# Layer B's channel-major products with the high and low halves side by side, and large tiles at multiples of 1024 bytes

## The chip, the core and the metric

The kernel runs on one core of a Trainium2 chip. A core has five engines that run their own instruction streams: TensorE (PE, matrix products into PSUM; its weight loads are shown as PEld), VectorE (DVE), ScalarE (ACT), GpSimd (POOL) and SyncE (SP, which issues the DMAs here). The metric is the device time of one execution in microseconds (us). The program is recorded through a tile layer which puts each engine's instructions in an order of its own making before they are built; each engine then runs its list strictly in that order and waits on semaphores.

## What is computed

A decoder trunk with two layers for 256 positions and a model width of 2048. Layer A is a Mamba-2 mixer. Behind it, one shared set of keys and values is made from the residual stream `x`. Layer B is a dilated windowed attention with three head groups, whose merged output is gated and projected. Only this part matters here:

```
x = layer A's output                                  # 256 x 2048
k, v = split(x @ kv_w, 2)                             # kv_w 2048 x 6144
h = x * (1 + scale) + shift                           # adaLN from c
q, z = split(h @ b_in_w, [3072])                      # b_in_w 2048 x 4096
o = merge of the three groups' attention(q, k, v)     # 256 x 1024
o = o * silu(z)
out = layer_norm(alpha * x + (1 + gate) * (o @ b_out_w))
```

All arrays are float32. TensorE's fast type for this is `float32r`, which keeps fewer bits, so the kernel splits each operand into a high half (`hi`, rounded to `float32r`) and a low half (`lo`, the remainder), and computes a product as three: hi·hi + hi·lo + lo·hi.

## The kernel before

**Weights.** Each weight matrix is laid out in pieces of 128 partitions x 1024 values (0.5 MB). `load_piece` (L84) issues the DMA of a piece into `raw` (6 buffers); `split` (L89) lets ScalarE copy it to `whi` (L92) and VectorE subtract to `wlo` (L94), 3 buffers each. In `wkv` and `wbin` a piece holds 512 columns for two row tiles of 128 (k = 2).

**Channel-major products.** `cm_quad` (L128) computes 512 output columns with channels on the partitions: 8 pieces, through `cm_piece` (L108). For each of the 16 row tiles and each of 4 blocks of 128 columns it issues three matmuls, all with 256 moving columns (the positions):

```
T.matmul(o, hi[:, k, c_], ahi[:, kt, :], ...)    # L118
T.matmul(o, hi[:, k, c_], alo[:, kt, :], ...)    # L119
T.matmul(o, lo[:, k, c_], ahi[:, kt, :], ...)    # L120
```

So a quad is 192 matmuls, each with a weight load of its own. Its four results lie in two PSUM tiles of 128 x 2 x 256, which ScalarE copies out with one 128x512 instruction each. **Token-major products** (`tm_chunk`, L152 to L154) have the activations as weights and `whi`/`wlo` as the moving operand, 512 columns at a time.

**The stages around the change**, with their place in the profiled execution (us from the span's start, read from the evictions and the matmuls):
- 560 to 743: layer A's output product (`tm_chunk` on `wout`, 768 matmuls of 512 columns), whose weights are `yhi` (tile name `actT`) and `ylo`; then layer norm.
- 758 to 826: `cm_quads` makes the keys of the first half of the heads, while `x_tiles` writes `xhi` and `xlo` (also `actT`).
- 826 to 904: three `cm_quad`s make the second half's keys, with `background(4, 9)`: four of layer B's adaLN columns (`araw`: a DMA of 1 MB and a dot product of 2.3 us on VectorE, L218) for every nine pieces.
- 904 to 1035: the values (`tm_chunk`). Then `xhi`/`xlo` are overwritten by the split of h.
- 1035 to 1262: `queries(0)`, `attend(0)`, `queries(1)`, `attend(1)`, `z_gate(0)`, `z_gate(1)` in program order: 6 + 2 quads on `wbin`. The tile layer moves matmuls of the next quad between those of `attend`, as filling.
- 1262 to the end: the output product on `wbout`, layer norm, and the output's DMAs.

Of the 26 quads' worth of channel-major work in the kernel, 11 are touched: 3 in the second keys' stage and 8 on `wbin`.

**Evictions**: `evict_k` (L665) and `queries` (L719) copy on ScalarE, two instructions for a quad; `z_gate` (L763) applies SiLU straight from PSUM, then VectorE multiplies (L764), and `split_act` splits the gated output on ScalarE (L175) and VectorE (L176) for the output product.

**Buffers and addresses.** The pool `act` has two buffers of 16 KB a partition, which hold in turn `hhi`/`hlo`, `yhi[0]`/`yhi[1]`, `xhi`/`xlo`, `gt`/`lnt`. In the program as built, `raw`, `whi`, `wlo` and `actT` start 128 bytes past a multiple of 1024; `ylo`, `kk`, `vt`, `qq` and the late split tiles `hi`/`lo` (L800) start 256 bytes past one. The split output of attention lies in the `kk` and `vt` buffers.

Of the kernel before, what the change touches and what calls it, by code (L numbers as in the profile page):

```python
# [9 lines left out]
F32 = mybir.dt.float32  # L10
F32R = mybir.dt.float32r
I32 = mybir.dt.int32
AF = mybir.ActivationFunctionType
ALU = mybir.AluOpType
# [4 lines left out]
P = 128  # L19
L = 256  # L20
D = 2048
KT = D // P
# [26 lines left out]
@with_exitstack  # L49
def trunk(ctx, tc, xT, x, c, par, cst, bias, lnrow, ada, wdt, win, wout, wkv, wbin, wbout, out):  # L50
    nc = tc.nc
# [3 lines left out]
    wp = ctx.enter_context(tc.tile_pool(name="wp", bufs=3))  # L55
    act = ctx.enter_context(tc.tile_pool(name="act", bufs=2))
    sm = ctx.enter_context(tc.tile_pool(name="sm", bufs=2))
# [12 lines left out]
    nc.sync.dma_start(prm, par)  # L70
    cc = cons.tile([P, NCONST], F32, name="cc")

    def pv(name):
# [58 lines left out]
    def cm_quad(src, ahi, alo, rate=(0, 1), k0=0):  # L132
# [4 lines left out]
        return ps  # L137

    def tiles(ps):
        return [ps[n // 2][:, n % 2, :] for n in range(4)]  # L140
# [37 lines left out]

    sm.tile([P, 40], F32, name="pad", bufs=1)
    magic = cons.tile([P, 2], I32, name="magic")  # L180
# [69 lines left out]

    hhi = act.tile([P, KT, L], F32R, name="actT")
    hlo = act.tile([P, KT, L], F32R, name="actT")

    with ExitStack() as cA:
# [14 lines left out]
        with ExitStack() as cS:  # L269
# [63 lines left out]
            with ExitStack() as c0:  # L333
# [73 lines left out]
                for i, (k, q) in enumerate(order):  # L407
# [5 lines left out]
                    z = k >= 0 and kinds[k] == "z"  # L413
# [152 lines left out]
        pn = cA.enter_context(tc.tile_pool(name="pn", bufs=1, reuse_waits="tile"))  # L566
        yhi = [act.tile([P, KT, L], F32R, name="actT") for _ in range(2)]
        ylo = {g: pn.tile([P, 4, L], F32R, name=f"ylo{g}") for g in (0, 1, 2, 3, 4, 7, 5, 6)}
# [68 lines left out]

    xhi, xlo = (act.tile([P, KT, L], F32R, name="actT") for _ in range(2))
    pb = ctx.enter_context(tc.tile_pool(name="pb", bufs=1))
# [23 lines left out]
    def evict_k(hq, g, ps):  # L663
        for w in range(2):
            S.activation(kk[hq][:, g, 2 * w:2 * w + 2, :], ps[w], AF.Copy)  # L665

    with ExitStack() as cL:
# [9 lines left out]
        with tc.issue_after(nb_last.ins):  # L677
            queue(pl, cols1[16:])
            jobs.append(lambda: gate_out(1))
            for g in range(NG):  # L680
                evict_k(1, g, cm_quad(wkv[2 * g + 1], xhi, xlo, rate=R))
            for hq in range(2):
                for g in range(NG):
                    ps = tm_chunk(wkv[6 + 2 * g + hq], hx, lx, rate=R)
                    for b in range(2):
                        S.activation(vt[hq][:, g, b, :], ps[b], AF.Copy)
            drain()
# [26 lines left out]
    def queries(hq):  # L714
        qq = pc2.tile([P, 12, L], F32, name="qq").rearrange("p (g i) l -> p g i l", g=NG)
        for g in range(NG):
            ps = cm_quad(wbin[2 * g + hq], xhi, xlo, rate=R)
            for w in range(2):
                S.activation(qq[:, g, 2 * w:2 * w + 2, :], ps[w], AF.Copy)  # L719
        return qq  # L720
# [39 lines left out]
    def z_gate(hq, qq):  # L760
        pz = cm_quad(wbin[6 + hq], xhi, xlo, rate=R)
        for w in range(2):
            S.activation(qq[:, 1, 2 * w:2 * w + 2, :], pz[w], AF.Silu)  # L763
        V.tensor_tensor(qq[:, 0], qq[:, 0], qq[:, 1], op=ALU.mult)  # L764
# [13 lines left out]

    gt = act.tile([P, 2, D], F32, name="actT")
    bcast(gt[:, 0, :], gated[1])  # L780
    lnt = act.tile([P, 2, D], F32, name="actT")
    for i in range(2):
# [53 lines left out]
def _layout(x, c, ada_w, ada_b, ln_g, ln_b, a_in_w, a_conv_w, a_conv_b, a_dt_bias,  # L836
# [27 lines left out]
    for g, (win_, dil) in enumerate(((128, 1), (512, 4), (2048, 16))):  # L864
# [13 lines left out]
        "ada": ada, "wdt": _dt(dt), "win": win,  # L878
        "wout": _pieces(a_out_w[0]), "wkv": _pieces(kv_w), "wbin": _pieces(b_in_w[0]), "wbout": _pieces(b_out_w[0]),
    }  # L880
# [20 lines left out]
```

## Time and profile before

| | before |
|---|---|
| median of 3 runs | 1321.53 us (1319.25 to 1325.56) |
| the profiled execution | 1324.63 us, of it the span of all instructions 1322.8 us |
| mean granted TensorE clock | 0.989 |
| channel-major matmuls, L118, L119, L120 | 1664 each, mean 285 to 287 ns |
| DMA traffic | 335.94 MB, mean 254 GB/s |

How to read it: a matmul's duration covers its whole way through the array, so that neighbours overlap; what a matmul costs in a dense stretch is the distance from its start to the next one's start, which is called its pitch here. In a table of windows, each engine's column gives the busy time and, behind x, the number of instructions that touch the window. In a group's row the busy time and the mean duration stand first, then the engine's idle time just before those instructions and what ended it.

### The profile page before, as it was taken

The numbers are of one execution on the slowest core, as the hardware profiler recorded it, in microseconds if no ns is written. First come the engines' busy times: TensorE is split into PE (matmuls) and PEld (weight loads), VectorE is DVE, ScalarE is ACT, GpSimd is POOL, SyncE is SP. The second block draws the span as 40 slices with busy tenths as digits, with TensorE's granted clock in tenths as the row PEclk, the third lists the DMA queues.
The fourth block names the chain that finished last, engine by engine and source line by source line (L and its number), as shares of the span: only waits on it lengthen the run. The fifth ranks groups of instructions, "written<-read, shape, count | busy, mean of one in ns | idle before, by whom it ended". The sixth has DMA issues, their size and how long they took to land.

```text
span 1322.8 us, 20650 instructions
## 1 busy us (share of the span) xinstructions
PE 1255.0 (95%) x8082; PEld 1133.5 (86%) x8082; DVE 1013.2 (77%) x1403; ACT 700.1 (53%) x1000; POOL 26.6 (2%) x20
## 2 busy tenths in 40 slices
PE   3799999999999999999999799999999999999995
PEld 3689988899989899777888699998888999999984
DVE  6889786999996788889765577877877647648577
ACT  3354478757766677854333444444445545445451
POOL 0000000000000000000000043000000000000000
PEclk9999999999999999999999899999999999999998
DMA  9999757777856555488966574898897553352471
GB/s 386 423 421 421 285 211 256 263 263 286 303 202 228 175 176 176 158 285 329 400 224 207 195 236 166 318 405 339 342 392 282 210 186 116 126 190 84 157 271 64
DMA packets 80450, 335.94 MB, mean 254 GB/s; under 512 B 8960, under 2 KB 9056, under 8 KB 67552
## 3 DMA queue, kind: packets, MB, share of 16 engines
q1 hardware_dynamic: 80352, 334.62, 68.1%
q8 instruction: 63, 1.03, 0.3%
q14 instruction: 35, 0.29, 0.1%
HBM read 332.41 MB, written 2.18 MB: 253 GB/s over the span
## 4 chain that ended last, share of the span: by engine, by line
PE 79%; DVE 10%; DMA 5%; ACT 3%; issue 2%; SPq 0%; ACTq 0%; DVEq 0%
PE acc L120 13%; PE acc L118 13%; PE acc L119 13%; PE acc L153 12%; PE acc L154 11%; PE acc L152 11%; DMA araw<-in_ada 4%; DVE wlo L94 3%; DVE araw L218 2%; PE py L530 2%; PE aux L732 1%; DVE cacc L287 1%; ACT whi L92 1%; PE po L756 1%; PE po L746 1%
## 5 line engine op out<-in xcount | busy, mean ns | idle before, releaser
L94 DVE TENSOR_TENSOR wlo<-raw,whi 128x1024 fp32r<-128x1024 f32 x394 | 486.1, 1241 | 239.0 <-ACT whi L92 236.2
L92 ACT ACTIVATE whi<-raw 128x1024 fp32r<-128x1024 f32 x394 | 414.9, 1057 | 415.7 <-PE acc L119 185.8
L118 PE MATMUL acc<-actT,whi 128*128 128x256 f32 x1664 | 474.5, 287 | 5.9 <-ACT whi L92 4.4
L120 PE MATMUL acc<-actT,wlo 128*128 128x256 f32 x1664 | 472.4, 287 | 6.2 <-DVE wlo L94 6.0
L119 PE MATMUL acc<-actT,whi 128*128 128x256 f32 x1664 | 472.9, 285 | 0.0
L118 PEld LDWEIGHTS acc<-actT,whi 128*128 128x128 f32 x1664 | 321.4, 194 | 8.3 <-ACT whi L92 5.6
L120 PEld LDWEIGHTS acc<-actT,wlo 128*128 128x128 f32 x1664 | 319.8, 193 | 9.1 <-DVE wlo L94 8.9
L119 PEld LDWEIGHTS acc<-actT,whi 128*128 128x128 f32 x1664 | 321.4, 193 | 0.5
L152 PE MATMUL acc<-whi,actT 128*128 128x512 f32 x704 | 272.0, 395 | 22.4 <-ACT actT L361 20.1
L153 PE MATMUL acc<-wlo,actT 128*128 128x512 f32 x704 | 278.6, 396 | 4.4 <-DVE wlo L94 4.3
L218 DVE SCALAR_TENSOR_TENSOR araw<-araw,cb__72 128x2048 f32<-128x2048 f32 x96 | 219.4, 2287 | 14.7 <-DMA araw<-in_ada 14.5
L152 PEld LDWEIGHTS acc<-whi,actT 128*128 128x128 f32 x704 | 133.0, 190 | 51.2 <-ACT actT L361 20.1
L154 PE MATMUL acc<-whi,actT 128*128 128x512 f32 x448 | 175.1, 391 | 0.0
L153 PEld LDWEIGHTS acc<-wlo,actT 128*128 128x128 f32 x704 | 132.6, 188 | 35.9 <-DVE wlo L94 8.3
L154 PE MATMUL acc<-whi,ylo 128*128 128x512 f32 x256 | 102.2, 400 | 0.0
L154 PEld LDWEIGHTS acc<-whi,actT 128*128 128x128 f32 x448 | 84.4, 188 | 16.8
L154 PEld LDWEIGHTS acc<-whi,ylo 128*128 128x128 f32 x256 | 48.0, 188 | 9.6
L287 DVE SCALAR_TENSOR_TENSOR cacc<-acc,prm,cacc 128x253 f32<-128x253 f32 (+2 forms) x96 | 42.3, 477 | 7.9 <-ACT cacc L284 7.5
L489 ACT ACTIVATE seg<-cbc,cumT 128x128 f32<-128x128 f32 x128 | 40.6, 388 | 11.5 <-PE py L530 11.5
L530 PEld LDWEIGHTS py<-xd,seg 128*128 128x128 f32 x256 | 30.7, 192 | 6.5 <-DVE xd L502 3.6
L530 PE MATMUL py<-xd,seg 128*128 128x64 f32 x256 | 30.5, 273 | 2.0 <-DVE xd L502 2.0
L702 POOL TENSOR_TENSOR u<-u,lnr 128x512 f32<-128x512 f32 x8 | 13.3, 1686 | 795.2 <-DMA lnr<-in_lnrow 763.7
(196 smaller groups left out, 927.0 us busy)
## 6 DMA issues: line engine op xcount, KB each, us to landing
araw<-in_ada SPq DMA_DIRECT2D x96, 1024.0 KB, 7.5
raw<-in_win SPq DMA_DIRECT2D x160, 512.0 KB, 5.0
raw<-in_wkv SPq DMA_DIRECT2D x96, 512.0 KB, 6.5
raw<-in_wout SPq DMA_DIRECT2D x64, 512.0 KB, 4.6
raw<-in_wbin SPq DMA_DIRECT2D x64, 512.0 KB, 3.3
cbc<-cumd SPq DMA_DIRECT2D x16, 512.0 KB, 5.4
raw<-in_wbout SPq DMA_DIRECT2D x16, 512.0 KB, 3.8
xt<-in_xT SPq DMA_DIRECT2D x8, 256.0 KB, 10.2
```

The source lines that it names most:

```text
L92: S.activation(hi, raw, AF.Copy)
L94: latest[0] = V.tensor_tensor(lo, raw, hi.bitcast(F32), op=ALU.subtract)
L118: T.matmul(o, hi[:, k, c_], ahi[:, kt, :], start=first, stop=False, skip_group_check=True)
L119: T.matmul(o, hi[:, k, c_], alo[:, kt, :], start=False, stop=False, skip_group_check=True)
L120: T.matmul(o, lo[:, k, c_], ahi[:, kt, :], start=False, stop=kt == k1 - 1, skip_group_check=True)
L152: T.matmul(ps[b], h_, hi[:, k, :], start=kt == k0, stop=False)
L153: T.matmul(ps[b], h_, lo[:, k, :], start=False, stop=False)
L154: T.matmul(ps[b], l_, hi[:, k, :], start=False, stop=kt == k1 - 1)
L218: V.scalar_tensor_tensor(raw, raw, 1.0, cb_, op0=ALU.mult, op1=ALU.mult, accum_out=mod[layer][:, ct, j:j + 1])
L287: V.scalar_tensor_tensor(acc[:, o:], ps[:, :L - o], w[:, j:j + 1], acc[:, o:], op0=ALU.mult, op1=ALU.add)
L489: S.activation(seg[:, hh, b, :], cbc[:, hh, b, :], AF.Relu, bias=cumT[:, b, h0 + hh:h0 + hh + 1], scale=-1.0)
L530: T.matmul(py[:, e_], segs[hh // 4][:, hh % 4, b, :], xd[:, b, e_], start=True, stop=True)
```

## The change

Three things are changed together.

1. A new `cm_wide` replaces `cm_quad` in the second keys' stage, in `queries` and in `z_gate`. It computes 256 output columns (a quad becomes two of them). `xhi` and `xlo` lie side by side in one tile `xp`, so that one matmul with `hi` as weights streams both (512 moving columns) into the two halves of a PSUM tile; a second one adds lo·hi (256 columns) to the first half. For 64 pairs a quad, three matmuls become two. The two halves must then be added: for each of the two PSUM tiles ScalarE copies one half out (128x256) and VectorE adds the other (128x256). `z_gate` applies SiLU afterwards, on the sum in SBUF.
2. The pieces for it hold 256 columns for four row tiles (`_pieces(w, 256, 4)`), as many bytes as before; the second keys' weights become an input of their own, `wk1`.
3. The pool `act` gets one buffer of 32 KB in place of two of 16 KB, with tiles that hold both halves; a pad of 896 bytes in `cons` and a smaller one in `sm` move the large tiles. As built, `raw`, `whi`, `wlo`, `actT`, `y`, `ylo`, `kk`, `vt`, `qq`, `hi`/`lo` all start at multiples of 1024 bytes.

The two programs' instruction lists as built have the same order on each engine up to the end of the first keys' stage. SP's list is the same throughout but for the source of the second keys' pieces.

```diff
-    act = ctx.enter_context(tc.tile_pool(name="act", bufs=2))
+    act = ctx.enter_context(tc.tile_pool(name="act", bufs=1))
...
+    cons.tile([P, 224], F32, name="pad")
...
+    def cm_wide(src, dst, rate=(0, 1)):
+        ps = acc_pair()
+        for q in range(KT // 4):
+            hi, lo = (t.rearrange("p k n -> p (k n)").rearrange("p (k n) -> p k n", k=4)
+                      for t in split(load_piece(src[q])))
+            for k in range(4):
+                kt = 4 * q + k
+                for n in range(2):
+                    c_ = slice(n * P, n * P + P)
+                    T.matmul(ps[n], hi[:, k, c_], xp[:, kt], start=kt == 0, stop=False, skip_group_check=True)
+                    T.matmul(ps[n][:, 0, :], lo[:, k, c_], xhi[:, kt, :], start=False, stop=kt == KT - 1,
+                             skip_group_check=True)
+            background(*rate)
+        for n in range(2):
+            S.activation(dst[:, n, :], ps[n][:, 1, :], AF.Copy)
+            V.tensor_tensor(dst[:, n, :], ps[n][:, 0, :], dst[:, n, :], op=ALU.add)
...
-    sm.tile([P, 40], F32, name="pad", bufs=1)
+    sm.tile([P, 8], F32, name="pad", bufs=1)
...
-    hhi = act.tile([P, KT, L], F32R, name="actT")
-    hlo = act.tile([P, KT, L], F32R, name="actT")
+    hp = act.tile([P, 2, KT, L], F32R, name="actT")
+    hhi, hlo = hp[:, 0], hp[:, 1]
...
-        yhi = [act.tile([P, KT, L], F32R, name="actT") for _ in range(2)]
+        yp = act.tile([P, 2, KT, L], F32R, name="actT")
+        yhi = [yp[:, 0], yp[:, 1]]
...
-    xhi, xlo = (act.tile([P, KT, L], F32R, name="actT") for _ in range(2))
+    xp = act.tile([P, KT, 2, L], F32R, name="actT")
+    xhi, xlo = xp[:, :, 0, :], xp[:, :, 1, :]
...
-                evict_k(1, g, cm_quad(wkv[2 * g + 1], xhi, xlo, rate=R))
+                for w in range(2):
+                    cm_wide(wk1[2 * g + w], kk[1][:, g, 2 * w:2 * w + 2, :], rate=R)
...
-            ps = cm_quad(wbin[2 * g + hq], xhi, xlo, rate=R)
             for w in range(2):
-                S.activation(qq[:, g, 2 * w:2 * w + 2, :], ps[w], AF.Copy)
+                cm_wide(wbin[2 * (2 * g + hq) + w], qq[:, g, 2 * w:2 * w + 2, :])
...
-        pz = cm_quad(wbin[6 + hq], xhi, xlo, rate=R)
         for w in range(2):
-            S.activation(qq[:, 1, 2 * w:2 * w + 2, :], pz[w], AF.Silu)
+            z = qq[:, 1, 2 * w:2 * w + 2, :]
+            cm_wide(wbin[2 * (6 + hq) + w], z)
+            S.activation(z, z, AF.Silu)
...
-    gt = act.tile([P, 2, D], F32, name="actT")
+    gl = act.tile([P, 2, 2, D], F32, name="actT")
+    gt, lnt = gl[:, 0], gl[:, 1]
...
-    lnt = act.tile([P, 2, D], F32, name="actT")
...
-        "wout": _pieces(a_out_w[0]), "wkv": _pieces(kv_w), "wbin": _pieces(b_in_w[0]), "wbout": _pieces(b_out_w[0]),
+        "wout": _pieces(a_out_w[0]), "wkv": _pieces(kv_w), "wbin": _pieces(b_in_w[0], 256, 4),
+        "wk1": _pieces(kv_w[:, :3072].reshape(D, 3, 2, 512)[:, :, 1].reshape(D, 1536), 256, 4), "wbout": _pieces(b_out_w[0]),
```

More of the change, by code (lines that the diff above doesn't have):

```diff
@@ L49, in trunk @@
 @with_exitstack
-def trunk(ctx, tc, xT, x, c, par, cst, bias, lnrow, ada, wdt, win, wout, wkv, wbin, wbout, out):
+def trunk(ctx, tc, xT, x, c, par, cst, bias, lnrow, ada, wdt, win, wout, wkv, wk1, wbin, wbout, out):
     nc = tc.nc
```

## The prediction

> **What bounds the kernel now.** I read the page first: its busy shares, its slices and the chain.
>
> ```profile
> PE 1255.0 (95%) x8082; PEld 1133.5 (86%) x8082; DVE 1013.2 (77%) x1403; ACT 700.1 (53%) x1000; POOL 26.6 (2%) x20
> GB/s 386 423 421 421 285 211 256 263 263 286 303 202 228 175 176 176 158 285 329 400 224 207 195 236 166 318 405 339 342 392 282 210 186 116 126 190 84 157 271 64
> PE 79%; DVE 10%; DMA 5%; ACT 3%; issue 2%; SPq 0%; ACTq 0%; DVEq 0%
> ```
>
> TensorE is busy 95% of the span and holds 79% of the chain that ended last. A 95% says nothing yet about the stages that are changed, so I asked for the busy times by stage: the first three rows are the second keys' stage (it ends at 904), the others run from the first query products to the last gate product.
>
> ```profile
> core 0: us, PE busy (x) PEld busy (x) DVE busy (x) ACT busy (x) POOL busy (x), PEclk, DMA share, GB/s
> 826.00:840.00 14.00, 13.36 (x112) 13.16 (x111) 11.15 (x11) 8.54 (x11) 0.00 (x0) 1.00 0.79 273
> 840.00:860.00 20.00, 19.60 (x164) 19.40 (x163) 17.82 (x16) 6.27 (x7) 0.00 (x0) 1.00 0.90 348
> 860.00:904.00 44.00, 44.00 (x366) 43.91 (x366) 34.54 (x31) 19.07 (x20) 0.00 (x0) 1.00 0.95 380
> ...
> 1037.00:1103.00 66.00, 66.00 (x552) 66.00 (x551) 29.78 (x26) 26.58 (x28) 0.00 (x0) 1.00 0.57 198
> 1103.00:1142.00 39.00, 38.93 (x277) 35.26 (x276) 33.45 (x89) 19.80 (x41) 0.00 (x0) 1.00 0.26 94
> 1142.00:1194.00 52.00, 52.00 (x435) 52.00 (x434) 22.49 (x19) 21.36 (x23) 0.00 (x0) 1.00 0.49 174
> 1194.00:1238.00 44.00, 43.90 (x317) 39.86 (x316) 34.79 (x90) 20.94 (x43) 0.00 (x0) 1.00 0.26 90
> 1238.00:1262.00 24.00, 24.00 (x203) 24.00 (x202) 13.04 (x11) 11.62 (x12) 0.00 (x0) 1.00 0.52 188
> ```
>
> In these rows TensorE idles 1.2 us in all, at full granted clock (1.00). So what a matmul less is worth is its pitch. VectorE is the second in line: 89% (17.82 of 20) while the adaLN columns are worked off, 86% and 79% under `attend`, 45% (29.78 of 66) in the plain query products. A saving on TensorE is real in the last kind of stage, and can be eaten by VectorE in the first two.
>
> The pitch comes from dense windows of one kind each:
>
> ```profile
> 930.00:1010.00 80.00, 80.00 (x354) 66.15 (x353) 65.39 (x59) 33.72 (x35) 0.00 (x0) 1.00 0.91 361
> 640.00:740.00 100.00, 100.00 (x435) 81.84 (x434) 58.14 (x56) 38.40 (x37) 0.00 (x0) 1.00 0.71 253
> 1040.00:1100.00 60.00, 60.00 (x502) 60.00 (x501) 26.10 (x23) 24.34 (x25) 0.00 (x0) 1.00 0.56 193
> 1270.00:1284.00 14.00, 14.00 (x62) 11.36 (x61) 12.27 (x14) 8.60 (x9) 0.00 (x0) 1.00 0.87 332
> ```
>
> About two of each count began before the window. The 256-column matmuls of the queries (third row): 60 / 500 = 120 ns. The 512-column ones of the values (first row): 80 / 352 = 227 ns. From the two: 107 ns for each 256 columns, and 13 ns for each matmul whatever its width (2 x 120 - 227 = 13). The two other rows are the output products of layers A and B: 100 / 433 = 231 ns and 14 / 60 = 233 ns, for the same shape as the 227.
>
> **The change part by part.**
>
> *Fewer, wider matmuls.* The streamed columns stay the same (512 + 256 in place of 3 x 256). In each of 11 quads x 64 pairs = 704 places one matmul and its weight load go, so 704 x 13 ns = 9.2 us, with the unrounded 2 x 120 - 226.7 = 13.3 ns 9.4 us. By stage: 3 quads in the second keys' stage, 192 x 13.3 = 2.5 us; 8 quads on `wbin`, 512 x 13.3 = 6.8 us. What the trace does not show is a 512-column matmul and a 256-column one in turn, with a weight load under each. Bounds: a pair costs 227 + 120 = 347 ns if each keeps its pitch, 360 if the fixed parts do not fall, and 320 (3 x 107) if they vanish, so 0 to 28 us are saved; a loss I leave out, since three matmuls in a row added to one place of PSUM before as well. I take 347: in the 120 ns stretches a weight load fits under a 256-column matmul already, and the same loads stand under both shapes.
>
> The Trainium skill, "TensorE: Matmul & The Clock Gate", section "Back-to-back issue gap", gives for a warm clock N / 2.4 + 2.5 ns from one matmul's start to the next, that is a fixed part of 2.5 ns where the rows above show 13. By it the 704 matmuls would be worth 1.8 us. The row's 13 decides.
>
> *Evictions.* For a quad two ScalarE copies of 128x512 from PSUM go; four of 128x256 and four VectorE additions come. Nearest rows: the copy in `queries`, a ScalarE copy of 128x256 out of PSUM, VectorE on 128x256 out of PSUM.
>
> ```profile
> L719 ACT ACTIVATE qq<-acc 128x512 f32<-128x512 f32 x12 | 7.0, 587 | 7.3 <-PE acc L120 7.3
> L752 ACT ACTIVATE pT<-po 128x256 f32<-128x256 f32 x16 | 6.1, 381 | 9.5 <-PE po L746 9.5
> L758 DVE COPY qq<-po 128x256 f32<-128x256 f32 x8 | 3.4, 423 | 5.8 <-PE po L757 5.7
> L94 DVE TENSOR_TENSOR wlo<-raw,whi 128x1024 fp32r<-128x1024 f32 x394 | 486.1, 1241 | 239.0 <-ACT whi L92 236.2
> L92 ACT ACTIVATE whi<-raw 128x1024 fp32r<-128x1024 f32 x394 | 414.9, 1057 | 415.7 <-PE acc L119 185.8 <-PE acc L154 177.7 <-DMA raw<-in_win 17.1
> L218 DVE SCALAR_TENSOR_TENSOR araw<-araw,cb__72 128x2048 f32<-128x2048 f32 x96 | 219.4, 2287 | 14.7 <-DMA araw<-in_ada 14.5
> L218 DVE DVE_READ_ACCUMULATOR araw<-araw,cb__72 128x1 f32 x96 | 8.0, 84 | 0.0
> ```
>
> ScalarE: 4 x 0.38 - 2 x 0.59 = +0.3 us a quad. VectorE: 4 x 0.42 = +1.7 us a quad. Behind each wide product the lists as built have: copy, weight split, copy on ScalarE; addition, split, addition on VectorE. When the product ends, two further pieces are already split, 2 x 16 matmuls x 173 ns = 5.5 us of TensorE work. The third piece's `lo` is ready after 0.4 (copy) + 1.06 (`whi`) + 1.24 (`wlo`) + 0.2 allowed for the steps between engines = 2.9 us. So in the query and gate stages the evictions cost nothing; 2.6 us of slack hide them. Each wide product has its own pair of PSUM tiles and the next one 11 us of work (64 x 173 ns), so no accumulator is late either.
>
> *Second keys' stage.* Here VectorE has, over 24 pieces, 24 x 1.24 + some 11 columns x 2.37 (the dot product and its accumulator's read) + 12 x 0.42 = 61 us, against 192 x 0.347 = 66.6 us of TensorE, and each of the six pairs of additions stands in line with the splits behind it: VectorE waits there for the product's end and two copies, up to 0.9 us each time. That is 61 + 5 = 66, no slack at all. Bounds: nothing lost if the additions find the product finished, 6 x 0.9 = 5.4 us if each wait comes in full. I take 1.5 us, since after 860 VectorE had 9 of 44 us free. The DMA queue carries the same bytes in 4% less time: 380 x 1.04 = 395 GB/s, below the 421 to 423 of the second to fourth slices.
>
> *Under `attend`.* VectorE gets about two additions in each of the two stages. ScalarE gets two more table loads: in the list as built the first SiLU stands between the exponentials of the last head, with a load before it and one behind.
>
> ```profile
> L763 ACT ACT_TABLE_LOAD  x1: 1283/1283/1283, 1237.8 to 1237.8; - x1
> L763 ACT ACTIVATE qq<-acc x4: 579/597/597, 1239.1 to 1263.6; 128x512 f32<-128x512 f32 x4
> ```
>
> That puts 2 x 1.28 + 0.6 = 3.2 us ahead of the last exponential. In front of the transposes that wait for it TensorE's list has 33 wide matmuls (33 x 173 ns = 5.7 us) where it had 27 narrow ones (3.2 us), so nearly all of it is hidden; the splits behind it on ScalarE are what could be late. From 0 to 3.2 us plus 4 x 0.42; I take 0.8 us for both `attend` stages.
>
> *The last gate.* Its chain to the output product was: SiLU twice (one split between them), multiply, split.
>
> ```profile
> 1262.07 0.60 ACT L763 ACTIVATE qq<-acc 128x512 f32<-128x512 f32 x1 [1.22 <-PE acc L120]
> ...
> 1267.81 1.22 DVE L176 TENSOR_TENSOR vt<-qq,kk 128x1024 fp32r<-128x1024 f32 x1
> ```
>
> 7.0 us, just covered by the first half of the output product. Now a copy, an addition and a VectorE split enter: 0.42 + 0.42 + 1.24 less the SiLU and wait they replace; by the lists some 7.7 us. I take 0.6 us (0 to 2).
>
> *Addresses.* Where moving operand and weights start at the same remainder of 1024 bytes, the 512-column pitch is 227 (`whi` and `actT`, both 128). Where they differ it is 231 to 233: `whi` 128 against `ylo` 256 in layer A's output product, and against `kk`/`vt` 256 in the first half of layer B's. Behind the change all are at 0. If the difference is the cause, 768 x 4 + 96 x 6 ns = 3.6 us go. Bounds: 0, if it is something else about those products, and a loss if the common remainder 0 is a bad one (a rival). I take 3.5.
>
> The Trainium skill, "SBUF — State Buffer", section "Who interferes with whom", gives TensorE two independent read ports, one for the moving operand and one for the weights, and lets it wait for nobody; by that the addresses would change nothing. No run here shows yet which holds.
>
> *Nothing else moves.* The order up to the end of the first keys' stage is the same on every engine; the single `act` tile is reused only after products that read both halves to their end.
>
> **The sum.** -9.4 - 3.5 + 1.5 + 0.8 + 0.6 = -10.0 us. The profiled execution took 1324.63 us (span 1322.8 and 1.8 around it), 3.1 over the median of the runs; 1324.6 would become 1314.6, and the median 1321.53 becomes **1311.5 us**, 0.76% less.
>
> **Rivals.**
> 1. *Addresses do nothing*: what slows the two output products is something else about them, and it stays: 1311.5 + 3.5 = 1315.0. For it: only two products show it. Against: all rows of this shape sort by the remainder. 12%. (The independent ports of the Trainium skill's "SBUF — State Buffer" would have it so.)
> 2. *The fixed part does not fall*: a narrow matmul behind a wide one takes 133 ns and a pair 360, so 1311.5 + 9.4 = 1321. For it: no such pair is in the trace. Against: the 13 ns stand under both widths. 6%. (By the Trainium skill's 2.5 ns a matmul it would be 1319.)
> 3. *VectorE takes TensorE's place* in the second keys' stage and under `attend`: with 5.4 for 1.5 and 3.2 + 1.7 for 0.8, so 1311.5 + 8 = 1319.5. For it: 89% and 86% busy before the additions come. 12%.
> 4. *Slower.* Bringing all tiles to one remainder makes moving reads and weight loads collide in every product, by the 4 to 6 ns that the unequal pairs show. The split products have these matmuls:
>
> ```profile
> L118 PE MATMUL acc<-actT,whi 128*128 128x256 f32 x1664 | 474.5, 287 | 5.9 <-ACT whi L92 4.4
> L152 PE MATMUL acc<-whi,actT 128*128 128x512 f32 x704 | 272.0, 395 | 22.4 <-ACT actT L361 20.1
> ```
>
>    3 x 1664 + 3 x 704 - 704 = 6400, x 6 ns = 38 us on top of rival 1's 1315: 1353. It is slower by more than 0.5% from 2.0 ns a matmul (6.5 that the rest gains and 6.6, over 6400). Against: pairs with equal remainders are the fast ones. 5%.
> 5. *Faster by far:* addresses also set the 13 ns; half of it gone is 6400 x 6.5 = 42 us, 1270. Against: at equal remainders 128 and 256 the pitch is the same, 227. 3%.
>
> **How the numbers follow.** The forecast has 62%, from 1304 (no costs, and runs as spread as before) to 1317. About 0.5% (6.6 us) is what a measurement tells from no change. Faster: nearly all of the forecast, half of rival 1, rival 5: 67%. Same: the rest of 1 and 2 and most of 3: 26%. Slower: 4 and the worst of 3: 7%. The range 1304 to 1320 takes in the forecast, rival 1 and part of 3, and leaves out about 20%.
>
> **What would show it.** Right: pairs of L152 and L153 at 227 and 120 ns; a `wbin` quad 22.2 us long in place of 23.0; layer A's output product at 227 ns a matmul, so 3 us shorter; VectorE near 95% between 830 and 860 with TensorE idle for 2 to 3 us; two table loads more. Wrong: a pitch of 133 behind a wide matmul (rival 2), gaps on TensorE released by `wlo` or the additions in every quad (rival 3), or the first layer's pitches of 120 and 227 moved at all (rivals 4 and 5).

## The result, and the profile after

| | before | after |
|---|---|---|
| median | 1322.61 us (1319.25 to 1325.56, 6 runs) | 1312.99 us (1310.91 to 1315.7, 6 runs) |
| ratio | | 0.9929, 95% interval 0.991 to 0.9949 |
| profiled execution, its span | 1324.63, 1322.8 us | 1312.58, 1310.8 us |

The changed kernel is 0.7% faster; the forecast was 1311.5 us, with a range from 1304 to 1320. First the page of the changed kernel: busy shares, the chain that ended last (its first row), and the groups that answer to those shown of before. Line numbers are each kernel's own; `cm_quad`'s matmuls are now L120 to L122, the wide ones L152 and L153, those of the output products L173 to L175.

```profile
PE 1241.7 (95%) x7378; PEld 1091.6 (83%) x7378; DVE 1027.8 (78%) x1447; ACT 704.7 (54%) x1028; POOL 26.4 (2%) x20
PE 77%; DVE 10%; DMA 6%; ACT 4%; issue 3%; SPq 0%; ACTq 0%; DVEq 0%
L120 PE MATMUL acc<-actT,whi 128*128 128x256 f32 x960 | 272.6, 287 | 6.2 <-ACT whi L94 4.7
L152 PE MATMUL acc<-actT,whi 128*128 128x512 f32 x704 | 250.1, 397 | 0.0
L153 PE MATMUL acc<-actT,wlo 128*128 128x256 f32 x704 | 201.3, 286 | 0.9 <-DVE wlo L96 0.9
```

There are 704 matmuls fewer (8082 less 7378), TensorE is busy 13 us less, and its share of the span is 95% as before: the kernel has become shorter along with its bound. The last row also says that the wide products waited 0.9 us for low halves in the whole run, so the additions on VectorE did not become the bound.

Where the time went is read from instructions that mark the stages; these rows give the first and the last start of each group. Before:

```profile
L577 PE MATMUL aux<-cc,y x64: 270/272/332, 557.9 to 607.1; 128*128 128x128 f32 x64
L646 PE MATMUL aux<-cc,u x32: 270/272/476, 755.8 to 815.3; 128*128 128x128 f32 x32
L665 ACT ACTIVATE kk<-acc x12: 576/597/598, 826.4 to 903.6; 128x512 f32<-128x512 f32 x12
L686 ACT ACTIVATE vt<-acc x12: 573/600/602, 924.7 to 1034.8; 128x512 f32<-128x512 f32 x12
L152 PE MATMUL acc<-whi,kk x32: 390/393/404, 1262.6 to 1284.3; 128*128 128x512 f32 x32
```

And after:

```profile
L599 PE MATMUL aux<-cc,y x64: 270/272/332, 556.0 to 605.5; 128*128 128x128 f32 x64
L669 PE MATMUL aux<-cc,u x32: 270/272/474, 751.7 to 811.3; 128*128 128x128 f32 x32
L688 ACT ACTIVATE kk<-acc x6: 577/589/598, 822.4 to 829.8; 128x512 f32<-128x512 f32 x6
L157 ACT ACTIVATE kk<-acc x12: 365/384/386, 840.7 to 897.6; 128x256 f32<-128x256 f32 x12
L710 ACT ACTIVATE vt<-acc x12: 572/598/599, 919.1 to 1029.2; 128x512 f32<-128x512 f32 x12
L173 PE MATMUL acc<-whi,kk x32: 389/389/504, 1250.7 to 1272.4; 128*128 128x512 f32 x32
```

From the marks come the lengths of the stages. The table gives them for the experiments too, from the same marks in their traces (us):

| | up to the last `y` transpose | layer A's output product | first keys | second keys | values | queries, attend, gates | output product to the end |
|---|---|---|---|---|---|---|---|
| before | 607.1 | 148.7 | 70.6 | 77.1 | 131.2 | 227.8 | 60.3 |
| after | 605.5 | 146.2 | 70.7 | 75.2 | 131.6 | 221.5 | 60.1 |
| e1 wide, old addresses | 604.3 | 148.7 | 70.8 | 75.8 | 131.6 | 221.1 | 60.6 |
| e2 addresses alone | 603.9 | 146.3 | 71.5 | 76.3 | 131.2 | 227.8 | 59.8 |
| e3 three narrow, new layout | 604.6 | 146.3 | 71.4 | 78.6 | 131.2 | 226.8 | 60.2 |
| e5 two wide, two narrow | 605.0 | 146.3 | 70.8 | 74.3 | 131.6 | 219.9 | 61.5 |
| e7 without the additions | 605.8 | 146.2 | 70.9 | 74.2 | 131.6 | 220.9 | 59.8 |
| e8 one SiLU | 604.1 | 146.2 | 70.8 | 75.8 | 131.6 | 221.8 | 60.1 |
| e9 by piece | 606.1 | 146.2 | 70.7 | 74.9 | 131.6 | 220.1 | 59.8 |
| e10 the change again | 605.6 | 146.2 | 71.4 | 74.9 | 131.7 | 221.3 | 60.1 |
| e12 unequal remainders | 604.7 | 148.7 | 71.1 | 76.5 | 131.6 | 221.5 | 60.6 |

Read the first column first: no instruction in it is changed by any of these kernels (about 52 of the 256 `ylo` products of layer A start in it, whose changed addresses are worth some 0.2 us there), and yet it varies by 3 us (by 4 with the kernels not in the table), about as much as the runs of one kernel do. Layer A's output product, the values and the queries' stage repeat to 0.1 to 0.7 us where the instructions are the same. The first keys vary by 1.1 us, and the second keys, with VectorE near its limit, by 1.6: 74.9 to 76.5 in after, e1, e8, e10 and e12, which issue the same instructions there. So most stages tell more here than a median, but each is one execution, and a difference in the second keys' stage has to be large to count. Of the 12.0 us by which the span fell, 1.6 lie in the first column; the rest is 10.4, of it 2.5 in layer A's output product, 2.0 (before rounding) in the second keys' stage, and 6.3 in the queries, `attend` and the gates.

Windows in dense stretches of the changed kernel: layer A's output product, the first queries, the second ones.

```profile
core 0: us, PE busy (x) PEld busy (x) DVE busy (x) ACT busy (x) POOL busy (x), PEclk, DMA share, GB/s
640.00:740.00 100.00, 100.00 (x443) 82.81 (x442) 59.38 (x56) 39.22 (x37) 0.00 (x0) 1.00 0.78 257
1040.00:1090.00 50.00, 50.00 (x285) 43.37 (x284) 25.42 (x28) 21.67 (x28) 0.00 (x0) 1.00 0.64 194
1143.00:1182.00 39.00, 39.00 (x227) 34.41 (x226) 19.46 (x21) 16.57 (x21) 0.00 (x0) 1.00 0.62 189
```

In the first row 443 matmuls stand where 435 stood: less the two that began before, 100 / 441 = 227 ns. The two others have the same shapes and the same clock, 1.00, and yet differ. The evictions give the pair's pitch exactly, since from the first copy of one wide product to that of the third after it lie 96 pairs. Copies between 1050 and 1086, and between 1150 and 1185:

```profile
L157 ACT ACTIVATE qq<-acc x7: 374/383/383, 1051.1 to 1085.0; 128x256 f32<-128x256 f32 x7
```

```profile
L157 ACT ACTIVATE qq<-acc x7: 378/383/385, 1151.2 to 1184.5; 128x256 f32<-128x256 f32 x7
```

33.9 / 96 = 353 ns, and 33.3 / 96 = 347 ns. The 347 is the sum of the forecast's 227 + 120. The 353 was in no part of it. A stretch of the trace at 353 shows how a pair divides; columns are the start, the duration, and the matmul:

```profile
1050.21 0.40 PE L152 MATMUL acc<-actT,whi 128*128 128x512 f32 x1
1050.45 0.28 PE L153 MATMUL acc<-actT,wlo 128*128 128x256 f32 x1
1050.57 0.40 PE L152 MATMUL acc<-actT,whi 128*128 128x512 f32 x1
1050.81 0.28 PE L153 MATMUL acc<-actT,wlo 128*128 128x256 f32 x1
1050.92 0.40 PE L152 MATMUL acc<-actT,whi 128*128 128x512 f32 x1
1051.16 0.28 PE L153 MATMUL acc<-actT,wlo 128*128 128x256 f32 x1
1051.28 0.40 PE L152 MATMUL acc<-actT,whi 128*128 128x512 f32 x1
```

The narrow matmul starts 0.24 us behind the wide one, and the next wide one 0.11 to 0.12 later. In the mean of these stretches the two distances are 237 and 117 ns where a pair takes 353 (1050 to 1085), and 230 and 117 ns where it takes 347 (1145 to 1182). So neither part has its price of the prediction's dense windows, only the 347 has their sum, and what grows in the slower pattern is the distance behind the wide matmul.

### The profile page after: what moved, and what is told of

Its sections match the earlier page's. It is cut to its first block, busy times and chain, and to the rows that moved or that the text cites. A ratio compares the mean times of both kernels' runs of the same rounds, so it can differ in the third digit from the quotient of the medians.

```text
span 1310.8 us, 19308 instructions
## 1 busy us (share of the span) xinstructions
PE 1241.7 (95%) x7378; PEld 1091.6 (83%) x7378; DVE 1027.8 (78%) x1447; ACT 704.7 (54%) x1028; POOL 26.4 (2%) x20
## 4 chain that ended last, share of the span: by engine, by line
PE 77%; DVE 10%; DMA 6%; ACT 4%; issue 3%; SPq 0%; ACTq 0%; DVEq 0%
PE acc L152 11%; PE acc L174 11%; PE acc L175 11%; PE acc L173 11%; PE acc L122 7%; PE acc L120 7%; PE acc L121 7%; PE acc L153 6%; DMA araw<-in_ada 5%; DVE wlo L96 3%; DVE araw L239 2%; PE py L551 2%; DVE cacc L308 1%; ACT whi L94 1%; PE aux L755 1%
## 5 line engine op out<-in xcount | busy, mean ns | idle before, releaser
L173 PE MATMUL acc<-whi,actT 128*128 128x512 f32 x704 | 271.6, 394 | 22.8 <-ACT actT L382 20.6
L120 PE MATMUL acc<-actT,whi 128*128 128x256 f32 x960 | 272.6, 287 | 6.2 <-ACT whi L94 4.7
L122 PE MATMUL acc<-actT,wlo 128*128 128x256 f32 x960 | 269.8, 286 | 5.1 <-DVE wlo L96 5.0
L121 PE MATMUL acc<-actT,whi 128*128 128x256 f32 x960 | 271.6, 284 | 0.0
L152 PE MATMUL acc<-actT,whi 128*128 128x512 f32 x704 | 250.1, 397 | 0.0
L153 PE MATMUL acc<-actT,wlo 128*128 128x256 f32 x704 | 201.3, 286 | 0.9 <-DVE wlo L96 0.9
L120 PEld LDWEIGHTS acc<-actT,whi 128*128 128x128 f32 x960 | 185.6, 194 | 8.3 <-ACT whi L94 5.9
L122 PEld LDWEIGHTS acc<-actT,wlo 128*128 128x128 f32 x960 | 183.6, 193 | 7.2 <-DVE wlo L96 7.2
L121 PEld LDWEIGHTS acc<-actT,whi 128*128 128x128 f32 x960 | 185.6, 193 | 0.4
L175 PE MATMUL acc<-whi,actT 128*128 128x512 f32 x448 | 175.1, 391 | 0.0
L173 PEld LDWEIGHTS acc<-whi,actT 128*128 128x128 f32 x704 | 132.0, 188 | 50.8 <-ACT actT L382 20.6
L152 PEld LDWEIGHTS acc<-actT,whi 128*128 128x128 f32 x704 | 132.1, 188 | 29.3
L153 PEld LDWEIGHTS acc<-actT,wlo 128*128 128x128 f32 x704 | 133.2, 189 | 2.4 <-DVE wlo L96 1.7
L175 PE MATMUL acc<-whi,ylo 128*128 128x512 f32 x256 | 100.5, 393 | 0.0
L175 PEld LDWEIGHTS acc<-whi,actT 128*128 128x128 f32 x448 | 84.4, 188 | 16.8
L175 PEld LDWEIGHTS acc<-whi,ylo 128*128 128x128 f32 x256 | 48.0, 188 | 9.6
```

The lines of the kernel that those rows point to most:

```text
L120: T.matmul(o, hi[:, k, c_], ahi[:, kt, :], start=first, stop=False, skip_group_check=True)
L121: T.matmul(o, hi[:, k, c_], alo[:, kt, :], start=False, stop=False, skip_group_check=True)
L122: T.matmul(o, lo[:, k, c_], ahi[:, kt, :], start=False, stop=kt == k1 - 1, skip_group_check=True)
L152: T.matmul(ps[n], hi[:, k, c_], xp[:, kt], start=kt == 0, stop=False, skip_group_check=True)
L153: T.matmul(ps[n][:, 0, :], lo[:, k, c_], xhi[:, kt, :], start=False, stop=kt == KT - 1, skip_group_check=True)
L173: T.matmul(ps[b], h_, hi[:, k, :], start=kt == k0, stop=False)
```

## The experiments

All ratios are to the kernel before, run beside the experiment on the same chip.

**e1 and e2: each half of the change alone.** e1 is the changed kernel with the tiles at their old remainders (128 and 256 past a multiple of 1024 bytes):

```diff
-    cons.tile([P, 224], F32, name="pad")
...
-    sm.tile([P, 8], F32, name="pad", bufs=1)
+    sm.tile([P, 40], F32, name="pad", bufs=1)
```

> The change without its pads, so that the large tiles keep the remainders of the kernel before (128 bytes for the split weights and xp, 256 for ylo and the kk and vt buffers). Theory (704 matmuls fewer at 13.3 ns each, and the output products slowed by unequal remainders): about 1316 us, with layer A's output product at 231 ns a matmul as before and the wide pairs at 347 to 354 ns. Rival (addresses do nothing): 1313 us as the full change, and the output product at 227. Rival (the addresses do all of it): 1321 us.

Measured: 1316.35 us, ratio 0.9949 (0.9932 to 0.9966). Its window in layer A's output product has the old count, and the wide pairs are as in the changed kernel:

```profile
640.00:740.00 100.00, 100.00 (x435) 81.84 (x434) 57.46 (x55) 38.40 (x37) 0.00 (x0) 1.00 0.74 249
1040.00:1090.00 50.00, 50.00 (x285) 43.31 (x284) 25.83 (x28) 21.07 (x28) 0.00 (x0) 1.00 0.64 190
```

e2 is the kernel before with the two pads of the change and nothing else:

```diff
+    cons.tile([P, 224], F32, name="pad")
...
-    sm.tile([P, 40], F32, name="pad", bufs=1)
+    sm.tile([P, 8], F32, name="pad", bufs=1)
```

> The kernel before with only the two pads changed, so that all large tiles start at multiples of 1024 bytes; every product is narrow. Theory: 1322.6 - 3.5 = about 1319 us, layer A's output product at 227 ns a matmul in place of 231, and the narrow products at 120 as before. Rival (addresses do nothing): 1322.6 and 231. Rival (the multiples of 1024 make every product faster): below 1315.

Measured: 1319.63 us, ratio 0.997 (0.9959 to 0.9981). Here the output product has the new count, and the narrow matmuls keep their pitch of 50 / 417 = 120 ns:

```profile
640.00:740.00 100.00, 100.00 (x443) 82.81 (x442) 58.10 (x55) 39.20 (x37) 0.00 (x0) 1.00 0.73 253
1040.00:1090.00 50.00, 50.00 (x419) 50.00 (x418) 20.83 (x17) 20.86 (x22) 0.00 (x0) 1.00 0.57 184
```

The halves work on different matmuls and add up: 0.51% and 0.30% make 0.81%, with the whole at 0.71% (0.51 to 0.9). Rival 1 (addresses do nothing) and rival 4 (a common remainder collides) have fallen.

**e3: the new layout without the wide matmul.** Everything of the change stays, the evictions with additions too; only the 512-column matmul becomes two of 256.

```diff
-                    T.matmul(ps[n], hi[:, k, c_], xp[:, kt], start=kt == 0, stop=False, skip_group_check=True)
+                    T.matmul(ps[n][:, 0, :], hi[:, k, c_], xhi[:, kt, :], start=kt == 0, stop=False, skip_group_check=True)
+                    T.matmul(ps[n][:, 1, :], hi[:, k, c_], xlo[:, kt, :], start=False, stop=kt == KT - 1, skip_group_check=True)
```

> The changed kernel, with three matmuls of 256 columns again in the place of the 512 and the 256, into the same halves of PSUM; pieces, additions, addresses and tiles as in the change. Theory (what is gained lies in the fixed part of each matmul): 704 x 13 ns come back less the 6 ns by which part of the pairs run above 347, so 7 to 9 us above the change, 1320 to 1322, at 120 ns a matmul. Rival (the gain is of the new pieces, the evictions or the order): within 2 us of 1313.

Measured: 1319.01 us, ratio 0.997 (0.9959 to 0.9982), as e2. So by the medians the layout, the pieces of four row tiles and the new evictions cost nothing that the runs resolve, and what the changed kernel has on top is the wide matmul. The stages of the two traces say 1.7 us more for e3 than for e2 (+2.3, -1.0 and +0.4), but e3's profiled execution, 1320.92 us, lay 1.9 above its median and e2's, 1318.59 us, 1.0 below. By the medians the wide matmul is then worth 4 to 5 us: the changed kernel is 9.6 us below its own before, and 8.7 when run again (e10), where e3 is 4.5 below its own; the spread of the runs leaves that uncertain by some 3 us. In the second keys' stage (window 831 to 900) TensorE waits for low halves 2.0 us, as the row shows; in the changed kernel it was 0.9.

```profile
L154 PE MATMUL acc<-actT,wlo 128*128 128x256 f32 x184 | 52.5, 285 | 2.0 <-DVE wlo L96 2.0
```

**e4 and e12: which addresses matter.** e4 is the kernel before with other pads, so that all large tiles start 256 bytes past a multiple of 1024 (one execution):

```diff
+    cons.tile([P, 32], F32, name="pad")
...
-    sm.tile([P, 40], F32, name="pad", bufs=1)
+    sm.tile([P, 8], F32, name="pad", bufs=1)
```

> The kernel before with pads that put the split weights, the activations, ylo, kk and vt all 256 bytes past a multiple of 1024: equal remainders, but no multiples of 1024. Theory (unequal remainders slow a product): layer A's output product at 227 ns a matmul. Rival (only multiples of 1024, or of 512, are good): it stays at 231. Rival (chance decides which pattern a product falls into): either, with no rule.

Measured: 1322.09 us, and in the window that decides:

```profile
640.00:740.00 100.00, 100.00 (x443) 82.80 (x442) 60.02 (x57) 39.09 (x37) 0.00 (x0) 1.00 0.77 260
```

443 again. A common remainder is enough; multiples of 1024 have no merit of their own. (The single time says little: its first stretch alone took 608.0 us, 4.1 more than e2's; from there on the two spans differ by 0.6 us.) e12 goes the other way: the changed kernel with 128 bytes more ahead of `ylo`, `kk` and `vt`.

```diff
-    sm.tile([P, 8], F32, name="pad", bufs=1)
+    sm.tile([P, 40], F32, name="pad", bufs=1)
```

> The changed kernel with 128 bytes more ahead of the tiles of layer A's output operand, the keys and the values: these begin at 128 past a multiple of 1024 again, the weights and layer B's moving operand stay at 0. Theory (a difference of the two operands' remainders costs 4 to 6 ns on a 512-column matmul): layer A's output product goes from 227 back to 231 (435 matmuls in 100 us in place of 443) and the first half of layer B's from 227 to 231 or more, 3.5 us: 1316.5. Rival (only the remainders 128 beside 256 cost, 0 beside 128 does not; or it is not the addresses): 227 stays and the time stays at 1313.

Measured: 1315.93 us, ratio 0.995 (0.9937 to 0.9964).

```profile
640.00:740.00 100.00, 100.00 (x434) 81.88 (x433) 57.28 (x54) 38.39 (x37) 0.00 (x0) 1.00 0.72 246
```

100 / 432 = 231 ns: the loss is back with remainders 0 and 128 as it was with 128 and 256.

The 231 is a mean over unlike matmuls. In layer A's output product only every third matmul has unequal remainders, the one with `ylo` as weights (L154 of the kernel before):

```profile
659.78 0.39 PE L152 MATMUL acc<-whi,actT 128*128 128x512 f32 x1
660.00 0.40 PE L153 MATMUL acc<-wlo,actT 128*128 128x512 f32 x1
660.24 0.40 PE L154 MATMUL acc<-whi,ylo 128*128 128x512 f32 x1
660.47 0.39 PE L152 MATMUL acc<-whi,actT 128*128 128x512 f32 x1
```

In the mean of this stretch of before the three distances are 227 ns from L152 to L153, 233 to L154 and 234 to the next L152: the matmul with `ylo` and the one ahead of it cost 6 to 7 ns more each; the three take 693 ns, and 680 in the changed kernel. The remainder that counts is not that of 1024 bytes: every other group of three reads weights 512 bytes further on in the same tiles (`[:, b*P:b*P + P]`, b = 1), and both kinds of group take 693 ns before and 680 after. Only a difference of 128 bytes was seen to cost time.

**e5, e6, e9, e10, e11: where the 353 ns comes from.** e5 issues, for each row tile, both wide matmuls and then both narrow ones; e11 is the same kernel once more; e9 issues the eight wide ones of a piece and then its eight narrow ones; e6 puts the narrow one of each pair first; e10 is the changed kernel again, on the same chip as e9 and e11.

```diff
+                cs = [slice(n * P, n * P + P) for n in range(2)]
                 for n in range(2):
-                    c_ = slice(n * P, n * P + P)
-                    T.matmul(ps[n], hi[:, k, c_], xp[:, kt], start=kt == 0, stop=False, skip_group_check=True)
-                    T.matmul(ps[n][:, 0, :], lo[:, k, c_], xhi[:, kt, :], start=False, stop=kt == KT - 1,
+                    T.matmul(ps[n], hi[:, k, cs[n]], xp[:, kt], start=kt == 0, stop=False, skip_group_check=True)
+                for n in range(2):
+                    T.matmul(ps[n][:, 0, :], lo[:, k, cs[n]], xhi[:, kt, :], start=False, stop=kt == KT - 1,
                              skip_group_check=True)
```

> The changed kernel with the four matmuls of a row tile in another order: both 512-column ones, then both 256-column ones. In the changed kernel a wide pair takes 347 ns (230 + 117) in some stretches and 353 (120 + 236 + 113 + 233 + 117 + 241 over three pairs) in the others, some 400 of 704 pairs. Theory A: the 353 comes from the alternation of widths, each 512 standing behind a 256. Then the row tile takes 2 x 227 + 2 x 120 = 693 ns everywhere in place of up to 707, some 2.6 us less than the changed kernel: 1310.4. Theory B: the pattern goes by the stage (what else runs beside it) or by the number of column counts, not by the order; the time stays at 1313 and both pitches stay. Rival: a 256 behind a 256 costs more with its weights loaded under another 256: slower than 1313.

> The changed kernel with the 256-column matmul of each pair ahead of the 512-column one. The sequence of widths on TensorE is the same alternation, 256, 512, 256, 512; only the weights' source changes: the 512's weights come from the rounded high half again and the moving operand alone decides. Theory A (alternation of widths) and theory B (stage) both expect the same pitches as in the changed kernel, 347 in some stretches and 353 in others, and 1313. If it depends on which half is loaded for the first matmul of a row tile's k step, the share of 353 changes, by up to 2.6 us either way.

> The changed kernel with each piece's eight 512-column matmuls first and its eight 256-column ones behind them. Theory A (a wide and a narrow matmul in turn take 347 or 353 ns by the phase in which the stretch began; two of each kind in turn took 348.3 everywhere): runs of eight make the change of width rarer, a pair takes 8 x 226.7 + 8 x 120 = 2774 / 8 = 346.7 ns everywhere, some 1.1 us less than with two of each; and the low half of a piece is needed 1.8 us later, so the two stalls of the second keys' stage (1.1 and 0.7 us) go: 1309, 2 to 4 us below the changed kernel. Rival: it is not the alternation but the 13 ns of the narrow ones that differ; then 1310.7 as with two of each.

> The changed kernel as it is, beside the two other orders on the same chip. All theories: 1313.0 (1310.9 to 1315.7 so far). It is the measure for the two orders: theory A has them 2 and 3 to 4 us below it; the rival has no difference beyond the spread, since the 1310.74 of two of each came from four runs only.

> Two 512-column matmuls, then two 256-column ones, once more, beside the changed kernel on the same chip. Theory A: 348.3 ns for a pair in every stretch, 1.5 to 2 us less than the changed kernel. Rival: the same time as the changed kernel, the first four runs having been low by chance.

| | median, us | ratio (95%) |
|---|---|---|
| e5 | 1310.74 | 0.9907 (0.9893 to 0.9922) |
| e6 (one execution) | 1313.72 | |
| e9 | 1312.26 | 0.993 (0.9916 to 0.9944) |
| e10 | 1313.62 | 0.9932 (0.992 to 0.9944) |
| e11 | 1313.4 | 0.9936 (0.9925 to 0.9948) |

By the times no order differs from the changed kernel; e5's 1310.74 was not seen again in e11. The traces say more. e5 has one pitch in both query stages, 33.4 / 96 = 348 ns (copies between 1050 and 1084.3, then between 1149 and 1183.3):

```profile
L158 ACT ACTIVATE qq<-acc x7: 362/364/378, 1050.8 to 1084.2; 128x256 f32<-128x256 f32 x7
```

```profile
L158 ACT ACTIVATE qq<-acc x7: 362/366/377, 1149.8 to 1183.2; 128x256 f32<-128x256 f32 x7
```

So the 353 belongs to wide and narrow in turn (theory A, though the pair did not come down to its 346.7), and the stage as its cause (theory B) falls with e10, which is the same program as the changed kernel. In the second keys' stage that one ran most of these 96 pairs at 347 (copies between 852.8 and 886, by the first row: 33.2 / 96 = 346), e10 all of them at 353 (second row: 33.9 / 96):

```profile
L157 ACT ACTIVATE kk<-acc x7: 365/385/385, 852.7 to 885.9; 128x256 f32<-128x256 f32 x7
```

```profile
L157 ACT ACTIVATE kk<-acc x7: 383/383/386, 852.6 to 886.5; 128x256 f32<-128x256 f32 x7
```

Which of the two patterns a stretch has is thus not set by the instructions alone; in the traces it holds until TensorE is next interrupted. It is not plain chance either: the first queries, 191 pairs (1029 to 1096 us in the changed kernel), ran at 353 in all seven traces with wide and narrow in turn. e6 keeps both patterns, but its second queries run at 353 and its last gate products at 347, the reverse of the changed kernel. e9's forecast of 346.7 was missed (33.52 / 96 = 349 from the unrounded starts, between 1051 and 1085.2):

```profile
L161 ACT ACTIVATE qq<-acc x7: 363/363/378, 1051.5 to 1085.1; 128x256 f32<-128x256 f32 x7
```

Why did 348 against 353 not show in e5's and e11's times? The stages tell: the queries, `attend` and the gates take 219.9 us in place of 221.5, and the output product behind them 61.5 in place of 60.1. TensorE's row there (e5, 1249 to 1275) has 1.4 us of waits, where the changed kernel waits 0.2 us in all:

```profile
L174 PE MATMUL acc<-whi,kk 128*128 128x512 f32 x31 | 12.1, 396 | 1.4 <-ACT whi L94 1.2 <-ACT kk L197 0.2
```

The gain is given back at the last gate, where a split of `wbout` comes late. e9 has no such wait (59.8) and is 1.4 us under e10 by the medians; that is inside the spread. The by-row-tile order with the old one in the last product alone was not run.

**e7: what the additions cost.** The changed kernel, with the first half of the PSUM tile copied out and nothing added. It leaves out the hi·lo part of these products; TensorE's work is the same.

```diff
-            S.activation(dst[:, n, :], ps[n][:, 1, :], AF.Copy)
-            V.tensor_tensor(dst[:, n, :], ps[n][:, 0, :], dst[:, n, :], op=ALU.add)
+            S.activation(dst[:, n, :], ps[n][:, 0, :], AF.Copy)
```

> The changed kernel without the additions of the wide evictions: ScalarE copies the first half of the PSUM tile and VectorE adds nothing. It leaves the high x low product (the second half of the 512 columns) out of layer B's first keys' second half, queries and gates; TensorE's work is unchanged. It measures what the additions cost. The prediction's terms: 1.5 in the second keys' stage, some 0.5 of the 0.8 under attend, 0.4 of the last gate's 0.6; all in all 2.4 less than the changed kernel, 1310.6. Theory of the traces: the second keys' stage fell by 2.0 of the ideal 2.5 us, so the additions cost 0.5 there and nearly nothing elsewhere: 1312.5.

Measured: 1312.38 us, ratio 0.9926 (0.9908 to 0.9943): no difference from the changed kernel by the times. By the stages, against after and e10: second keys 1.0 and 0.7 us, queries to gates 0.6 and 0.4, the end 0.3: 1.4 to 1.9 in all. That is an upper bound: the last gate's some 70 pairs ran at 347 in e7 and at 353 in after and e10, which makes 0.5 us, and e6 and e9 have the same 59.8 us at the end although they add. In the second keys' stage (831 to 897) no wait of TensorE is left, the low halves' row included:

```profile
L153 PE MATMUL acc<-actT,wlo 128*128 128x256 f32 x188 | 52.4, 281 | 0.0
```

**e8: the extra table loads.** The first gate quad's SiLU is taken once, over both halves, behind its second wide product.

```diff
-            S.activation(z, z, AF.Silu)
+            if hq == 1:
+                S.activation(z, z, AF.Silu)
+        if hq == 0:
+            S.activation(qq[:, 1], qq[:, 1], AF.Silu)
```

> The changed kernel with the first gate quad's SiLU taken once over both halves, after the second wide product, so that two table loads of 1.28 us go (33 in place of 35). If the extra loads under attend cost what the prediction put there, some 0.3 to 0.8 us less than the changed kernel: 1312.4. If they are hidden by TensorE's wide matmuls: 1313.0, no difference. Against it: the single SiLU over 128x1024 stands later in ScalarE's list and may hold up a split: up to 1 us more.

Measured: 1312.85 us, ratio 0.9926 (0.9911 to 0.9941), and 221.8 us for the stage in place of 221.5 and 221.3. After had these loads, e8 one fewer in each row:

```profile
L763 ACT ACT_TABLE_LOAD x2 | 2.6, 1283 | 0.0
L787 ACT ACT_TABLE_LOAD x2 | 2.6, 1283 | 0.0
```

The two loads are hidden. The patterns of the pairs do not alter that: e8's second queries ran at 353 (132 pairs, 0.9 us more than in after) and its last gate at 347 (some 70 pairs, 0.5 us less), so that 221.8 would be 221.4 with after's.

## Why the prediction was right

The time was 1.5 us above the forecast, and the terms of its sum are these, each by the stages of single traces:

| term | forecast | measured | from |
|---|---|---|---|
| wide matmuls | -9.4 | -8.7 to -9.2, of it some 1.1 that TensorE waits less (2.0 and 0.9) | e3 to after and e10: second keys 78.6 to 75.2 and 74.9, queries to gates 226.8 to 221.5 and 221.3 |
| addresses | -3.5 | -2.9 | e2: 148.7 to 146.3, 60.3 to 59.8 |
| additions, second keys | +1.5 | +2.3 with narrow matmuls, +0.7 to +1.0 with wide ones | e2 to e3; e7 to e10 and after |
| `attend` | +0.8 | -1.0 | e2 to e3, 227.8 to 226.8 |
| last gate | +0.6 | +0.3 to +0.4 | e2 to after and e3 |
| sum | -10.0 | -10.4 | before to after, without the first stretch |

The steps from before to e2, to e3, to the changed kernel lead from one end to the other, so that -2.9 + 2.3 - 1.0 + 0.4 - 8.7 (or 9.2) = -9.9 (or -10.4) had to add up; it is no proof of each term. The closeness of the total is in part luck: the 353 ns pattern took 2.3 us that the forecast did not have, and `attend` and the second keys' stage together gave back about as much.

- *A fixed part of 13 ns for each matmul, of 704 of them*: right in kind. Where a wide and a narrow one follow each other undisturbed in the good pattern, a pair takes 347 ns, the sum of the forecast's 227 + 120, though its parts are 230 and 117. Its step "I take 347" failed for about half of the pairs, which take 353: there only 7 of the 13 ns are saved. In the trace some 340 pairs stand so outside `attend`: 340 x 6.7 ns = 2.3 us. So by the pitches the term is 9.4 - 2.3 = 7.1 us, between the 8.7 to 9.2 of the stages, which take in the shorter waits and all that was peculiar to e3's one trace, and the 4 to 5 of the medians; the runs do not fix it closer. Rival 2 (360) fell. By the Trainium skill's "TensorE: Matmul & The Clock Gate", section "Back-to-back issue gap", whose isolated gap has 2.5 ns for it, the term would have been 1.8 us; the traces disagree, since a pair takes 347 or 353 ns where three narrow matmuls took 3 x 120 = 360, which saves 7 to 13 ns and not 2.5.
- *Addresses*: the mechanism was right and is now shown from both sides, by e2 and e4 (equal remainders, 227) and by e1 and e12 (unequal, 231). The 4 ns that the forecast gave each of the 768 matmuls are the mean of 0, 6 and 7. By the stages the size came out 0.6 smaller, of which some 0.2 lie in the first column; by the medians of e2 it is 3.8 us. The forecast's other reading, two independent read ports by the Trainium skill's "SBUF — State Buffer", section "Who interferes with whom", would have left the time alone; what TensorE does here depends on where both operands lie. Which part of the path to memory they share is not shown.
- *Second keys' stage*: VectorE at 95% was right (18.92 of 20 below); TensorE's idle time of 2 to 3 us was not: 0.66 and 0.25 us in these two windows, 0.9, less than the 1.0 of before. The additions brought other waits, but no more of them.

```profile
826.00:840.00 14.00, 13.34 (x83) 11.77 (x83) 11.08 (x10) 6.77 (x8) 0.00 (x0) 1.00 0.79 295
840.00:860.00 20.00, 19.75 (x112) 16.91 (x112) 18.92 (x20) 8.52 (x11) 0.00 (x0) 1.00 0.96 371
```

- *Under `attend`*: the sign was wrong. The new layout took 1.0 us off even with narrow matmuls, and the table loads cost nothing (e8). It is not that TensorE waits less: it idled 0.2 us in this stage in e2 and 0.4 in e3. So the order in which the filling matmuls and those of `attend` follow each other has become cheaper by more than that; whether the finer evictions, four small ones in place of two, bring this order about was not tried by itself.
- *Last gate*: right in size, 0.3 to 0.4 for 0.6; that the additions are its cause is not shown, since e6 and e9 add as well and have 59.8 us as e2 has.
- *Rivals 3 and 5*: VectorE cost at most 1.9 us in all (e7), and no narrow pitch moved with the addresses (120 ns in e2), so both fell.

## What to carry to other kernels

A matmul's pitch, read from dense windows at two widths, gives what a matmul costs apart from its columns; with a fixed part of that size, streaming both halves through one weight load pays even when the columns stay the same, provided that the engine which adds the halves has room. Look at the addresses of both operands of a product as the program is built: tiles that began 128 bytes apart in their remainders cost 13 ns on each group of three matmuls, and an easy pad took that away. When medians differ by less than their spread, compare the lengths of stages between marks, and look in the stage behind for what is given back; but read from two executions of the same kernel first how far each stage repeats.

## What the runs showed of the hardware that was not expected

- Wide and narrow matmuls in turn have two steady patterns, 347 and 353 ns for a pair, in one and the same program at one and the same clock; two of each in turn have one, 348 ns, and eight of each 349 ns. In both patterns the next wide matmul starts 117 ns behind the narrow one; the narrow one starts 230 or 237 ns behind the wide one. What chooses between the two patterns beyond "where TensorE was last interrupted" stays open.
- In the token-major products a 512-column matmul costs 227 ns where the tiles of moving operand and weights start at the same remainder of 1024 bytes (0, 128 and 256 were seen), weights 512 bytes further on included. Where the weights are 128 bytes off (0 and 128, 128 and 256), it and the matmul ahead of it cost 232 to 234 ns. Equal tiles do not make every 512-column matmul that fast: the wide ones of e9, eight in a row, follow each other by 231 ns in the mean (1051 to 1085).
- The first 600 us, whose instructions no kernel here changes (addresses only), took 603.9 to 608.0 us in fourteen profiled executions, at mean clocks of 0.988 to 0.992.
